# Conv taps copied by transfers into four buffers, one shift sum per slice of the start by moving rows, and four modulation sums side by side, in a two-layer conditioned decoder trunk

## The chip, the cores and the metric

One core of a Trainium2 chip runs the whole program. The metric is device time in microseconds (us) of one execution, the median of three runs; smaller is better. TensorE is called PE (its weight loads PEld), VectorE DVE, ScalarE ACT, GpSimd POOL; SP only issues transfers.

## What is computed

One sequence of 256 tokens (2 tiles of 128), width 1024, two layers. All matrices are float32 and come from HBM once. Every sublayer is modulated: a vector c of 1024 goes through silu and, by `ada_w` (1024 x 9216 for each layer), gives a shift, a scale and a gate for each of the three sublayers.

```python
def swiglu_ffn(h, w_in, w_out):
    u = h @ w_in
    a, b = jnp.split(u, 2, axis=-1)
    return (jax.nn.silu(a) * b) @ w_out

def conformer_conv(h, w_pw1, b_pw1, w_dw, b_dw, ln_g, ln_b, w_pw2, b_pw2):
    u = h @ w_pw1 + b_pw1
    a, g = jnp.split(u, 2, axis=-1)
    u = a * jax.nn.sigmoid(g)
    u = depthwise causal convolution of u over time, 31 taps w_dw, + b_dw
    u = jax.nn.silu(layer_norm(u, ln_g, ln_b))
    return u @ w_pw2 + b_pw2

for i in range(2):
    mod = (silu(c) @ ada_w[i] + ada_b[i]).reshape(B, 3, 3, 1024)
    shift, scl, gate = mod[:, :, 0], mod[:, :, 1], mod[:, :, 2]
    pre = lambda z, j: rms_norm(z, norm_g[i, j]) * (1 + scl[:, j]) + shift[:, j]
    x = x + 0.5 * gate[:, 0] * swiglu_ffn(pre(x, 0), w_in[i, 0], w_out[i, 0])
    x = x + gate[:, 1] * mixer_i(pre(x, 1))        # layer 0: attention, layer 1: conv
    x = x + 0.5 * gate[:, 2] * swiglu_ffn(pre(x, 2), w_in[i, 1], w_out[i, 1])
```

## The kernel before

**Arithmetic.** Every large product is done in three passes of fp32r matmuls: a float32 operand is split into a rounded part (`whi`, `hh`, made by ACT) and a rest (`wlo`, `hl`, made by DVE), and hi*hi, lo*hi and hi*lo are added up in PSUM (`mm3`, L608 to L610).

**The stream.** `plan` writes one list of all weight pieces of 512 KB in the order in which they are used, with pieces of `ada_w` woven in. SP loads them (L203) into a ring of six `raw` buffers. `step` takes one piece: a weight piece is split by ACT (L243) and DVE (L218), a piece of `ada_w` is multiplied by silu(c) on DVE and added up over its rows in an accumulator `acc` of 128 x 512 (L279, L281). Only when a piece has been used is the next load issued. `block` stands before each group of matmuls and runs as many steps as the quota of the stage allows (`PUMP`, in the conv loop `PUMP_LOOP` = 5); `need` runs steps until a certain weight is split. There is no scheduler: each engine runs its instructions in the order in which the code emits them, and waits where an operand isn't there.

**Modulation sums.** A finished `acc` holds half a vector of 1024, still spread over 128 partitions. For a shift or a scale, `column_sum` (L322) sums it with four matmuls whose stationary operand is a 128 x 128 piece of `acc` and whose moving operand is one column of ones; `finish` (L333, L336) adds the bias on DVE. This happens 20 times, for five sublayers, two vectors, two halves. A gate goes through `row_sum` (L312, L313).

**The start.** The shift and scale of the first sublayer are needed at once, in four slices of 256 (`early_fold`, `early_sum`, q = 0 to 3). Of the four pieces of a slice DVE folds three (L477, L479). The fourth, the second half of the shift, goes through PE with the raw weights as the stationary operand (L499, four matmuls of one column for each 128 columns); L500 adds the folded parts.

**The conv.** Eight blocks b of 128 channels. Blocks 0 to 3 are computed with time on the partitions (`UT`, two times each) and turned (`across`), blocks 4 to 7 directly (`U`). `glu(b)` (L1009, L1010) writes 256 time steps of 128 channels into one of three buffers `ub`. `spread(b)` then makes `R[b]`: four groups g of 32 channels, each copied four times, shifted by 0 to 3 steps, onto the four quarters of the partitions; that is 16 copies of 32 x 284 elements, 11 by DVE (L1024) and 5 by ACT (L1022), with two `R` buffers. `wide(b)` (L963, POOL) lays the taps out as 32 x 32 diagonals, with two buffers `wd`. `C(b)` (L1033) is 32 matmuls of 32 output channels each, four groups in four column quarters of the array. `VT` turns the result back, `moments`, `norm` and `swish` do the layer norm and silu, and `O(t, j)` multiplies by `w_pw2`. In the loop over b a turn runs `glu(b+2)`, `C(b)`, `spread(b+2)`, `U(b+4)`, `wide(b+2)`, `VT(b-1)`.

## Time and profile before

| | |
|---|---|
| median of 3 runs | 1071.75 us (1071.41 to 1072.74) |
| the profiled execution's own time | 1072.88 us |
| its span | 1071.0 us |
| PE busy | 1038.3 us (97%) |
| DVE / ACT / POOL busy | 815.1 / 503.8 / 53.2 us |
| read from HBM | 248.24 MB, 233 GB/s over the span |

The span is the time from the first to the last instruction; some 1.9 us lie around it. A busy share is an average over stages: what an instruction is worth is read from its own stage, from what ends the waits there.

### The profile page before, as it was taken

Reading aid. Unit: us, or ns where it says so; the run is one execution under the profiler, and the core shown is the slowest. Engines: PE = TensorE matmul, PEld = TensorE weight load, DVE = VectorE, ACT = ScalarE, POOL = GpSimd, SP = SyncE. Lnnn points to the kernel's source line nnn. Section 1 sums busy time; section 2 is a strip of 40 time slices with the busy share of each in tenths; the row PEclk is TensorE's granted clock in tenths of the full one; section 3 lists DMA queues with packets and bytes.
Section 4 is the critical chain, followed back from the end, with each engine's and each line's share of the span. In section 5 each row is a group of like instructions: output and inputs, shape, how many; then the busy total and the mean of one; then the engine's idle time right before and its main releaser. Section 6 shows DMA issues by size and latency. Waiting matters only on the chain.

```text
span 1071.0 us, 14807 instructions
## 1 busy us (share of the span) xinstructions
PE 1038.3 (97%) x5522; PEld 853.5 (80%) x5522; DVE 815.1 (76%) x1267; ACT 503.8 (47%) x794; POOL 53.2 (5%) x83
## 2 busy tenths in 40 slices
PE   8999999999999999999999999999988799999998
PEld 6888888877777788888878888888867588888886
DVE  5878878878997798778568788776789768665643
ACT  3354444555676544344354444454555446434430
POOL 3000000001210000000020000000211100000000
PEclk8999999999999999999999999999988899999999
DMA  8979998948767399898728889885545227776711
GB/s 297 297 244 340 307 324 296 332 160 260 248 205 221 101 324 313 281 311 293 251 88 311 284 296 317 284 289 159 164 149 195 86 65 238 270 230 199 236 40 39
DMA packets 181692, 250.26 MB, mean 234 GB/s; under 512 B 8389, under 2 KB 132070, under 8 KB 181620
## 3 DMA queue, kind: packets, MB, share of 16 engines
q1 hardware_dynamic: 180784, 248.55, 69.6%
q0 software_dynamic: 688, 0.71, 0.3%
q8 instruction: 43, 0.70, 0.2%
q14 instruction: 29, 0.24, 0.1%
q10 hardware_dynamic: 148, 0.06, 0.0%
HBM read 248.24 MB, written 1.05 MB: 233 GB/s over the span
## 4 chain that ended last, share of the span: by engine, by line
PE 87%; DVE 8%; issue 2%; ACT 1%; DMA 1%; POOL 1%; SPq 0%; DVEq 0%; POOLq 0%; ACTq 0%
PE u L608 15%; PE u L610 15%; PE u L609 14%; PE y L608 11%; PE y L610 11%; PE y L609 11%; DVE R L1024 2%; DVE wlo L218 2%; PE m L686 2%; PE m L322 1%; PE m L1033 1%; DMA raw<-in_ada_w_dram 1%; PE m L499 1%; DVE x L545 1%; PE m L587 1%
## 5 line engine op out<-in xcount | busy, mean ns | idle before, releaser
L218 DVE TENSOR_TENSOR wlo<-raw,whi 128x1024 fp32r<-128x1024 f32 x320 | 382.4, 1224 | 31.2 <-ACT whi L243 31.0
L243 ACT ACTIVATE whi<-raw 128x1024 fp32r<-128x1024 f32 x320 | 328.5, 1054 | 164.2 <-DMA raw<-in_ffn_w_in_dram 97.7
L608 PE MATMUL u<-whi,hh 128*128 128x512 f32 x672 | 266.5, 397 | 0.0
L610 PE MATMUL u<-whi,hl 128*128 128x512 f32 x672 | 262.7, 391 | 0.0
L609 PE MATMUL u<-wlo,hh 128*128 128x512 f32 x672 | 261.8, 390 | 0.0
L281 DVE SCALAR_TENSOR_TENSOR acc<-raw,sc,acc 128x512 f32<-128x512 f32 x224 | 169.5, 757 | 5.6 <-DMA raw<-in_ada_w_dram 0.7
L610 PEld LDWEIGHTS u<-whi,hl 128*128 128x128 f32 x672 | 126.1, 188 | 28.4 <-DVE hl L603 1.2
L608 PEld LDWEIGHTS u<-whi,hh 128*128 128x128 f32 x672 | 126.3, 188 | 25.5 <-ACT hh L602 0.6
L609 PEld LDWEIGHTS u<-wlo,hh 128*128 128x128 f32 x672 | 126.4, 188 | 25.1
L608 PE MATMUL y<-whi,gh 128*128 128x512 f32 x352 | 138.8, 394 | 0.2 <-ACT gh L694 0.2
L610 PE MATMUL y<-whi,gl 128*128 128x512 f32 x352 | 137.3, 390 | 0.0
L609 PE MATMUL y<-wlo,gh 128*128 128x512 f32 x352 | 137.1, 389 | 0.0
L695 DVE TENSOR_TENSOR gl<-m,gh 128x512 fp32r<-128x512 f32 (+1 forms) x48 | 31.1, 647 | 93.0 <-ACT gh L694 92.8
L608 PE MATMUL y<-whi,hh 128*128 128x512 f32 (+1 forms) x256 | 98.2, 384 | 0.0
L609 PE MATMUL y<-wlo,hh 128*128 128x512 f32 (+1 forms) x256 | 94.9, 371 | 0.0
L610 PE MATMUL y<-whi,hl 128*128 128x512 f32 (+1 forms) x256 | 94.7, 370 | 0.0
L694 ACT ACTIVATE gh<-m 128x512 fp32r<-128x512 f32 (+1 forms) x48 | 27.0, 562 | 132.4 <-PE m L686 132.4
L656 ACT ACTIVATE sg<-u 128x256 f32<-128x256 f32 x84 | 32.1, 382 | 113.9 <-PE u L610 113.9
L610 PEld LDWEIGHTS y<-whi,gl 128*128 128x128 f32 x352 | 66.1, 188 | 14.6 <-DVE gl L695 0.4
L608 PEld LDWEIGHTS y<-whi,gh 128*128 128x128 f32 x352 | 66.1, 188 | 13.8 <-ACT gh L694 0.7
L609 PEld LDWEIGHTS y<-wlo,gh 128*128 128x128 f32 x352 | 66.1, 188 | 13.3
L657 DVE TENSOR_TENSOR g<-u,sg 128x256 f32<-128x256 f32 x84 | 35.5, 422 | 35.0 <-ACT sg L656 34.6
(157 smaller groups left out, 984.4 us busy)
## 6 DMA issues: line engine op xcount, KB each, us to landing
raw<-in_ffn_w_in_dram SPq DMA_DIRECT2D x164, 512.0 KB, 5.0
raw<-in_ada_w_dram SPq DMA_DIRECT2D x144, 512.0 KB, 5.0
raw<-in_ffn_w_out_dram SPq DMA_DIRECT2D x88, 512.0 KB, 5.1
raw<-in_attn_w_qkv_dram SPq DMA_DIRECT2D x24, 512.0 KB, 4.8
raw<-in_conv_w_pw_dram SPq DMA_DIRECT2D x24, 512.0 KB, 4.9
raw<-in_ffn_w_in_dram SPq DMA_DIRECT2D x24, 256.0 KB, 5.5
raw<-in_attn_w_o_dram SPq DMA_DIRECT2D x8, 512.0 KB, 4.6
gate<-in_ada_b_dram SPq DMA_DIRECT2D x6, 512.0 KB, 6.7
```

What stands on the lines that cost most here:

```text
L218: (eng or nc.vector).tensor_tensor(lo, raw, hi.bitcast(F32), op=ALU.subtract)
L243: self.nc.scalar.activation(hi, self.like(self.raws[i], hi), AF.Copy)
L281: nc.vector.scalar_tensor_tensor(dst, raw[:, i, :], self.sc[:, k : k + 1], dst, op0=ALU.mult, op1=ALU.add)
L608: nc.tensor.matmul(out, lh, rh, start=start, stop=False)
L609: nc.tensor.matmul(out, lh, rl, start=False, stop=False)
L610: nc.tensor.matmul(out, ll, rh, start=False, stop=stop)
L656: nc.scalar.activation(sg, ps[:, 0:256], AF.Silu)
L657: nc.vector.tensor_tensor(gs[c][:, t, :], ps[:, 256:512], sg, op=ALU.mult)
L686: nc.tensor.transpose(ps[:, o : o + P], g[:, t, k * P : k * P + P], self.ident)
L694: nc.scalar.activation(hi, src, AF.Copy)
L695: nc.vector.tensor_tensor(lo, src, hi.bitcast(F32), op=ALU.subtract)
L1024: nc.vector.tensor_copy(dst, src)
```

## The change

**Conv copies.** `spread` no longer runs on DVE and ACT: the 16 copies of a block become 16 transfers from SBUF to SBUF, eight issued by SP and eight by POOL. `R` and `ub` get four buffers, `wd` three. The order is new: all four of `glu(0..3)`, `spread(0..3)` and `wide(0..2)` stand before the loop, a turn of the loop runs `U(b+4)`, `glu(b+4)`, `C(b)`, `spread(b+4)`, `wide(b+3)`, and the last three blocks are computed for the first 128 time steps before the others. The weights of the conv come first in the stream, the pieces of `ada_w` for (1,2,0) behind them.

**The start.** DVE folds two of the four pieces (the scale). Both pieces of the shift go through PE with silu(c), repeated over 32 columns, as the stationary operand and the raw rows as the moving operand: eight matmuls of 32 x 256 in four column quarters. ACT copies the result (`br`), and two matmuls with the vector `pick` bring it onto the partitions. The two loads of x are issued one piece earlier each.

**Sums.** In the stages up to the third FFN, four finished accumulators are summed together: four matmuls with 32 columns of ones as the stationary operand and `acc` (512 columns) as the moving one, an ACT copy, and two blocks later four transposes (`columns_turn`). There are four such groups of four; the other four sums keep the old form. `acc` has five buffers there. The order of the vectors in the stream changes for this.

```diff
-            vec.acc = self.fp.tile([P, n], F32, name="acc", tag="acc", bufs=2)
+            vec.acc = self.fp.tile([P, n], F32, name="acc", tag="acc", bufs=bufs)
...
-                self.sums.append([3, self.column_sum, vec, dst, c0])
+                self.open.append((vec.number, vec, dst, c0))
+                self.pend.append(self.open[-1])
+                if self.phase > 3 or len(self.pend) == 4:
+                    self.sums.append([3, self.column_sums, self.pend])
+                    self.pend = []
...
+        m = 32 * len(accs)
+        for j, (_, vec, acc, c) in enumerate(accs):
+            nc.tensor.matmul(ps[32 * j : 32 * j + 32, :], self.ones.bitcast(F32)[:, 0:32], acc, start=True, stop=True)
+        rows = self.two.tile([P, 512], F32, name="rows", tag="sq", bufs=1)
+        nc.scalar.activation(rows[0:m, :], ps[0:m, :], AF.Copy)
+        self.sums.append([1, self.columns_turn, accs, rows])
+
+    def columns_turn(self, accs, rows):
...
         for i in range(4):
-            nc.tensor.matmul(ps[:, i : i + 1], acc[:, i * P : i * P + P], self.one, start=True, stop=True)
-        self.finish(vec, ps[:, 0:4], c)
+            nc.tensor.transpose(ps[:, i * P : i * P + m], rows[0:m, i * P : i * P + P], self.ident[0:m, 0:m])
...
+        for e, raw in enumerate(shift):
+            if not q:
                 idle(IDLE_SUMS)
...
+            for k in range(4):
+                nc.tensor.matmul(
+                    rows[32 * k : 32 * k + 32, 0:256], self.sc32[:, 4 * e + k, :], raw[:, k, :],
+                    start=e == 0, stop=e == 1,
+                )
+            self.issue()
+        br = self.two.tile([P, 256], F32, name="br", tag="sq", bufs=1)
+        nc.scalar.activation(br, rows[:, 0:256], AF.Copy)
...
-            R[b] = cp.tile([P, 4, 284], F32, name="R", tag="R", bufs=2)
+            u = ub[b % 4]
+            R[b] = cp.tile([P, 4, 284], F32, name="R", tag="R", bufs=4)
             for g in range(4):
                 for j in range(4):
-                    dst, src = R[b][32 * j : 32 * j + 32, g, :], u[32 * g : 32 * g + 32, j : j + 284]
-                    if 4 * g + j in (1, 4, 7, 10, 13):
-                        nc.scalar.activation(dst, src, AF.Copy)
-                    else:
-                        nc.vector.tensor_copy(dst, src)
+                    eng = nc.sync if (g + j) % 2 else nc.gpsimd
+                    eng.dma_start(R[b][32 * j : 32 * j + 32, g, :], u[32 * g : 32 * g + 32, j : j + 284])
...
-        for b in range(6):
-            if b >= 4:
-                self.block()
-            if b:
-                glu(b + 2)
+        for b in range(4):
+            U(b + 4)
+            glu(b + 4)
             C(b)
...
-            spread(b + 2)
-            if b + 4 < 8:
-                U(b + 4)
-            wide(b + 2)
+            spread(b + 4), wide(b + 3)
...
+        C(4), wide(7), VT(3)
+        self.need(self.pw2[3])
+        take(5)
+        C(5, 0, P), VT(4), self.block(), C(6, 0, P), VT(5, (0,)), C(7, 0, P), VT(6, (0,))
+        C(5, P, P), VT(7, (0,)), moments(0), norm(0, 0), norm(0, 1)
...
-    nc = _bacc.Bacc("TRN2", target_bir_lowering=False, num_devices=1)
+    nc = _bacc.Bacc("TRN2", target_bir_lowering=False, num_devices=1, dynamic_dma_scratch_size=8192)
```

POOL in the conv, from the load of the bias `b` to the powers of the layer norm. Before:

```order
L1100 DMA b_6575<-in_conv_b_pw_dram 128x1024
L963 TENSOR_TENSOR wd<-w_4927,mask 128x1024 x8
L1059 TENSOR_TENSOR lr_7683<-lr_7683,mhalf 128x1
L1059 TENSOR_TENSOR lr_7738<-lr_7738,mhalf 128x1
L564 TENSOR_TENSOR r_7860<-v_7859,mhalf 128x1
```

POOL in the same place, changed:

```order
L1077 DMA R<-ub_6535 32x284 x8
L1077 DMA R<-ub_6532 32x284 x8
L1019 TENSOR_TENSOR wd<-w_4906,mask 128x1024
L1077 DMA R<-ub_6533 32x284 x8
L1019 TENSOR_TENSOR wd<-w_4906,mask 128x1024
L1077 DMA R<-ub_6534 32x284 x8
L1019 TENSOR_TENSOR wd<-w_4906,mask 128x1024
L1077 DMA R<-ub_6535 32x284 x8
L1019 TENSOR_TENSOR wd<-w_4906,mask 128x1024 x2
L1111 TENSOR_TENSOR lr_7646<-lr_7646,mhalf 128x1
```

The eight tap layouts stood alone on POOL; now 64 transfers stand between them, eight ahead of each (the first three blocks, of the same pattern, are left out above), and the layouts of blocks 6 and 7 come last of all.

PE in the second slice of the start (q = 1), between two groups of the FFN's matmuls. Before:

```order
L500 MATMUL m<-one,acc 128x1 x2
L499 MATMUL m<-sc,raw 128x1 x4
L500 MATMUL m<-one,acc 128x1
L499 MATMUL m<-sc,raw 128x1 x4
L500 MATMUL m<-one,acc 128x1
L516 MATMUL m<-ident,z 128x128 x4
L608 MATMUL y<-whi,hh 128x512
```

PE in the same place, changed:

```order
L545 MATMUL m<-raw,sc_158 32x256 x8
L572 MATMUL m<-ident,z 128x128 x4
L535 MATMUL m<-one,acc 128x1 x2
L557 MATMUL m<-pick,br 128x1 x2
L664 MATMUL y<-whi,hh 128x512
```

Twelve matmuls of one column become eight of 256 columns and four of one column; the transposes of z now stand between the row sums and the matmuls that need ACT's copy of them.

## Rows read from the trace of the kernel before

**Rows 1.** The page, part 2: busy tenths of PE in 40 slices

```profile
PE   8999999999999999999999999999988799999998
```

**Rows 2.** Stretches: start:end, length, busy us by engine, PEclk, DMA share, GB/s

```profile
768.00:850.00 82.00, 68.22 (x845) 54.21 (x847) 71.99 (x130) 42.63 (x76) 11.74 (x6) 0.88 0.47 155
850.00:878.90 28.90, 27.37 (x174) 22.57 (x163) 19.25 (x42) 15.00 (x32) 1.66 (x3) 1.00 0.06 19
27.60:40.80 13.20, 13.20 (x69) 11.31 (x68) 11.14 (x22) 4.62 (x6) 0.00 (x0) 0.87 0.96 313
```

**Rows 3.** The chain that ended last, 767 to 856 us: start, us, what

```profile
767.04 0.38 ACT sg L1009
767.44 0.50 DVE ub L1010
...
780.04 0.58 PE u L608
...
852.04 0.64 PE m L1070 x4
...
855.32 0.34 PE y L608
```

**Rows 4.** A group of instructions: line, count | busy, mean ns | idle

```profile
L1024 DVE COPY R<-ub 32x284 f32<-32x284 f32 x88 | 32.6, 370 | 5.4 <-PE m L1033 3.5
```

**Rows 5.** PE in time, 764 to 800 us: start, us, instruction, tile, count

```profile
769.56 0.60 PE L1001 MATMUL u<-ident,z 128*128 128x128 f32 x4
...
788.46 3.66 PE L1033 MATMUL m<-R,wd 128*32 128x256 f32 x64
...
797.91 0.38 PE L1047 MATMUL y<-ident,v 128*128 128x128 f32 x2
```

**Rows 6.** The transfers of the taps, tile tq: ns min/median/max; us to landing

```profile
L931 POOL DMA_DIRECT2D tq<-in_conv_w_dw_dram x8: 551/551/618, 556.9 to 561.3; - x8
...
DMA to landing us min/median/max: 1.9/3.5/4.3
```

**Rows 7.** The stretch of the tap loads, columns as in rows 2

```profile
550.00:560.00 10.00, 10.00 (x50) 8.34 (x49) 8.31 (x14) 5.28 (x11) 3.54 (x8) 1.00 0.21 65
```

**Rows 8.** POOL in time around 830 us: one tap layout

```profile
830.13 1.98 POOL L963 TENSOR_TENSOR wd<-w,mask 128x1024 f32<-128x1024 f32 x1 [8.58 <-PE m L1033]
```

**Rows 9.** DVE in time around 810 and 830 us: two splits each

```profile
810.43 2.36 DVE L218 TENSOR_TENSOR wlo<-raw,whi 128x1024 fp32r<-128x1024 f32 x2
...
830.33 4.00 DVE L218 TENSOR_TENSOR wlo<-raw,whi 128x1024 fp32r<-128x1024 f32 x2
```

**Rows 10.** Transfers by line: issuing queue, KB each, median us to landing

```profile
ab<-in_ada_b_dram POOLq DMA_DIRECT2D x1, 36.0 KB, 5.7
```

**Rows 11.** The output's stores, tile x: ns min/median/max of one issue on SP

```profile
L547 SPq DMA_DIRECT2D out_dram<-x x6: 332/332/344, 1057.9 to 1068.3; - x6
```

**Rows 12.** The chain that ended last, whole span: sums and four transposes

```profile
118.23 0.44 PE m L686 x4
...
144.63 0.79 PE m L322 x8
...
263.68 0.98 PE m L322 x8
```

**Rows 13.** PE and ACT in time in the start, 0 to 56 us

```profile
10.43 1.65 PE L396 MATMUL y<-ones 128*128 128x512 f32 x4
...
16.61 0.56 PE L500 MATMUL m<-one,acc 128*128 128x1 f32 x2
...
27.65 0.50 PE L500 MATMUL m<-one,acc 128*128 128x1 f32 x4
...
28.09 1.06 ACT L243 ACTIVATE whi<-raw 128x1024 fp32r<-128x1024 f32 x1 [1.69 <-DMA raw<-in_ffn_w_in_dram]
...
30.63 0.47 PE L608 MATMUL y<-whi,hh 128*128 128x512 f32 x1
...
31.83 0.63 PE L609 MATMUL y<-wlo,hh 128*128 128x512 f32 x1
```

More of the change, by code (lines that the diff above doesn't have):

```diff
@@ L271, in ada_fold @@
         if k0 == 0:
-            if sum(job[1] == self.column_sum for job in self.sums) > 1:
+            bufs = 2 if self.phase > 3 else 5
+            if any(i <= self.naccs - bufs for i, *_ in self.open):
                 self.run_sums(True)
-            vec.acc = self.fp.tile([P, n], F32, name="acc", tag="acc", bufs=2)
+            vec.acc = self.fp.tile([P, n], F32, name="acc", tag="acc", bufs=bufs)
+            vec.number = self.naccs
+            self.naccs += 1
         dst = vec.acc
@@ L303, in run_sums @@
             job[0] -= 1
+        if force and self.pend:
+            self.sums.append([0, self.column_sums, self.pend])
+            self.pend = []
         while self.sums and (force or self.sums[0][0] < 0):
@@ L467, in early_fold @@
         nc = self.nc
-        accs = []
-        for e in range(3):
+        acc = self.fp.tile([P, 512], F32, name="acc", tag="acc", bufs=5)[:, 0:256]
+        shift = []
+        for e in range(4):
             raw = self.raws[self.taken].rearrange("p (k n) -> p k n", k=4)
-            if e != 1:
-                acc = self.fp.tile([P, 512], F32, name="acc", tag="acc", bufs=2)[:, 0:256]
-                accs.append(acc)
+            self.taken += 1
+            self.high = max(self.high, self.taken)
+            if e >= 2:
+                shift.append(raw)
+                continue
             for i in range(4):
-                k = 4 * (e % 2) + i
+                k = 4 * e + i
                 if k == 0:
@@ L1117, in conv @@
         e = evac(w[1])
-        glu(0), spread(0)
+        glu(0), spread(0), wide(0)
         UT(w[3][:, 256:], 3, 1)
```

124 lines of the change are left out of this document (70 added, 54 removed).

## The prediction

> **What bounds the kernel now.** I read the page's slices first. PE is busy in nine or more tenths of nearly every slice [rows 1]; outside the conv a us that PE doesn't spend is a us of the total, as long as DMA, DVE and ACT keep up. The dip around slice 31 is the conv, and the view by stretch says why: from 768 to 850 us PE works 68.2 of 82.0 us at a mean granted clock of 0.88, while DVE is busy 72.0 [rows 2]. The chain of waits there is a chain of DVE work: `glu` ends at 767.9, and PE's first `U` starts only at 780.04, behind DVE's copies of R, splits and three more `glu` [rows 3]. The copies alone are 32.6 us on DVE [rows 4], and ACT has five a block besides. So in the conv DVE is the bound, and PE pays twice, by waiting and by a lower clock after the waits.
>
> **The conv.** The stretch to compare runs from `glu(0)` (767.44) to the first matmul of O (855.32): 87.9 us [rows 3]. Of the changed order I work out two paths, PE's and POOL's.
>
> PE's path. UT(3,1) ends at 769.56 [rows 5], since nothing ahead of it changes its inputs. Then come ACT's copy of the result, sigmoid (0.38), `glu` (0.50) and the last `across`, which needs the bank that `glu(1)` frees: about 2.3 us, so U(4) starts near 771.9. One U takes 5.79 us (from the end of C at 788.46 + 3.66 to VT at 797.91), one C 3.66, a pair of VT about 0.31 [rows 5]. Four U are 23.2, eight blocks of C 29.3, eight pairs of VT 2.5, at the clock of those rows. The last C would end at 826.9. From the first transposes of `swish` to O it was 3.28 us [rows 3], and this chain stays. O would start at 830.2: a gain of 25.1.
>
> POOL's path. POOL has 64 transfers to issue and eight layouts to write. The nearest row to a transfer from SBUF to SBUF over 32 partitions is the load of the taps, also 32 partitions: 0.551 us of POOL each, landing after 1.9 to 4.3 [rows 6], while DVE was busy 8.3 of 10 us [rows 7]; I take 0.56. A layout is 1.98 [rows 8]. From 767.9 that is 64 x 0.56 + 8 x 1.98 = 51.7: the layout of block 7 is done at 819.6, and only then can C(7) start. Behind its start stand four half blocks (7.3) and VT (0.6): 827.5, so O at 830.8. Both paths end together, so POOL's price decides.
>
> One thing adds to it. With a layout on POOL, a pair of splits on DVE took 4.00 us, without one 2.36 [rows 8, 9]: DVE stood still for most of the layout. The other way round a layout must wait for the split in hand, on average half of 1.2 us; eight times that is 4.9, and O comes at 835.7. By the Trainium skill ("SBUF — State Buffer", SBUF: two separate sides) the engine that starts first holds a port pair shared by DVE and GpSimd for its whole instruction. By that rule the term would be between 0 and 9.8, and the trace agrees with the lock. Between 830.8 and 835.7 I take the middle, 833.2: **a gain of 22 us.**
>
> Bounds. The best is PE's path without any wait, 25. For the worst, POOL's code keeps eight transfers in flight and reuses a slot when the one eight back has landed. A load of 36 KB, the size of one copy (32 x 284 x 4 bytes), landed after 5.7 us on this queue [rows 10]; then a transfer costs 5.7 / 8 = 0.71, 64 x 0.15 = 9.6 more, and the gain is 10 (855.3 - 845.3). 0.56 is nearer, because the tap loads are several in a row over 32 partitions.
>
> What hides the rest. SP issues eight copies a block, about 0.33 us each [rows 11], 2.7 us in a turn of 9.5 (U + C), beside five loads. The first of the eight waits for `glu(b+4)` and for C(b), and all weight loads behind it on SP wait too; the ring of six raw pieces covers that, because the weights of the conv all come ahead of the copies of block 0, and those behind are wanted only at O and in the last FFN. DVE loses 32.6 us of copies in a stage where it was busy 72 of 82, so it is late no more: five splits of 1.2 us and a `glu` are 6.6 in a turn of 9.5. ACT gets five copies a block back. The slower clock goes with the waits it follows: from 850 on, with 1.5 us of idle, it was 1.00 [rows 2].
>
> **The sums.** A sum of one half vector takes PE 0.79 us, in the attention 0.98 [rows 12]. Sixteen sums go, twelve at 0.79 and four at 0.98: 13.4 us. A group of four needs four matmuls of 32 x 512, side by side. C is the same form: 32 matmuls of 256 columns, four abreast, in 3.66, so four of 512 cost 3.66 x 4 / 32 x 2 = 0.91; with four transposes (0.44 [rows 12]) a group is 1.35, four are 5.4. **Gain 8.0.** Were the four not to overlap, a group would be 3.66 + 0.44 = 4.1, a loss of 3; against this stands that C does overlap. ACT's copy of the sums has two blocks of PE work as cover. If that cover went, it would cost ACT's copy, under 1 us for each group. DVE's part is the same as before.
>
> **The start.** In slices 1 to 3 the sums and the transposes of z take PE 2.98 us (27.65 to 30.63 [rows 13]). Now: eight matmuls of 256 columns, 0.91 by the row of C, four transposes 0.44, eight instructions of one column 0.79: 2.14, or 0.8 less each, 2.5 together. Behind the old sums the clock fell: the matmul at 31.83 took 0.63 us [rows 13], and from 27.6 to 40.8 the granted clock is 0.87 [rows 2], 1.7 us lost. The same happens once more, after the last slice. The new sums keep more columns moving, so these 3.4 us may go. But DMA was busy 0.96 of this stretch [rows 2], and ACT's split at 28.09 had waited for its load [rows 13]: loads give a floor that I can't see past. Also PE must wait for ACT's copy `br` behind such a split. In slice 0 the shift saves PE time, but `idle` (1.65 us [rows 13]) now stands twice ahead of the last sums, which ended at 17.2. I take **3 us**, with bounds of -1 (slice 0 later by one idle, nothing else but 0.6) and 7.
>
> **Sum.** 22 + 8 + 3 = 33. The profiled execution took 1072.9 us (span 1071.0 and 1.9 around it); 1072.9 - 33 = 1039.9. The median is 1.1 below the profiled one, so 1038.8, rounded **1039**. The bounds give 1072.9 - 1.1 - (25 + 8 + 7) = 1032 and 1071.8 - (10 + 8 - 1) = 1055.
>
> **The rivals.**
> 1. Loads held back on SP. If the copies' waits for C(b) delay the weights, ACT's splits stand still in front of the sigmoid and of the evacuation of C, which PE needs. Three turns with 5 us each (one landing) take 15 of the conv's 22: 1054. For it: SP works in order. Against it: the ring is six deep and these weights aren't urgent.
> 2. POOL's slots. The change gives the transfers' descriptors an area of 8192 bytes. If it holds only four at a time, a transfer costs 3.5 / 4 = 0.88 [rows 6], 64 x 0.32 = 20.5 on top of 835.7: no gain in the conv is left, and the time is 1061. Against it: the tap loads followed each other at 0.55.
> 3. Slower: POOL's issue waits for DVE. If each issue, like a layout, has to wait for half a split, it costs 0.56 + 0.61 = 1.17; O comes at 835.7 + 39 = 874.7, the conv loses 19, and with 11 gained elsewhere the time is 1080. It decides from 1.04 us a transfer (835.7 + 64 x 0.48 = 866.4, 11 behind the old 855.3). Against it: 0.551 to 0.618 while the tap loads ran beside a busy DVE [rows 6, 7]. The Trainium skill ("SBUF — State Buffer", SBUF: two separate sides) speaks for it: a copy of float32 on DVE keeps GpSimd from writing descriptors, so that a transfer of about 620 ns takes about 3100. The loop of the changed kernel has hardly such copies left; no run here shows how it is with splits.
> 4. The sums don't overlap: 11 us less, 1050.
>
> **How the numbers follow.** Forecast (1030 to 1049) 0.62; rivals 1 and 4 or a slow landing (1049 to 1056) 0.17; rival 2 (1056 to 1069) 0.09; within 0.2%, about what a measurement of this kernel can tell from no change, 0.03; rival 3 0.09. Faster: 0.62 + 0.17 + 0.09 = 0.88. The range leaves out rivals 2 and 3 and the 0.03: 1030 to 1056.
>
> **What would show it.** Right: on POOL, transfers at 0.56 us back to back and the last layout near 820; PE between 772 and 828 nearly without idle at a granted clock near 1.00; O some 22 us earlier relative to the conv's start; four sums in about 0.9 us. Wrong: POOL's issues at 0.7 us or more, C waiting for R or `wd` (rivals 2, 3), ACT waiting for raw loads in the loop (rival 1), PE waiting for `br` or for splits in the first 55 us. A conv that takes as long as before would make the prediction wrong, whatever the sums do.

## The result, and the profile after

The changed kernel takes 1057.4 us in the median of 4 runs (1055.2 to 1060.7), the kernel before 1071.6 beside it: a ratio of 0.987, 95% interval 0.984 to 0.990. That is a gain of 14.2 us where 33 had been forecast, 1.4 us outside the range. Its profiled execution took 1057.27 us, of which 1055.5 is the span.

The slices of the page first (40 equal parts of the span, each digit the busy share in tenths; PEclk is TensorE's granted clock):

```profile
PE   8999999999999999999999999999995899999998
PEclk9999999999999999999999999999998999999999
```

The kernel before has, in the row of the clock:

```profile
PEclk8999999999999999999999999999988899999999
```

The first slice's dip is gone from the clock (9 in place of 8), and PE's hole, 887 in [rows 1], is now 58, in slices 30 and 31. By stretch (busy us of PE, PEld, DVE, ACT, POOL with the number of instructions, then granted clock, DMA share, GB/s):

```profile
0.00:30.00 30.00, 26.69 (x130) 18.58 (x131) 15.69 (x39) 11.73 (x22) 8.70 (x35) 0.94 0.90 302
755.00:800.00 45.00, 43.86 (x511) 35.98 (x513) 27.79 (x24) 14.49 (x22) 34.17 (x53) 1.00 0.67 203
800.00:830.00 30.00, 14.41 (x266) 10.80 (x262) 20.61 (x21) 7.80 (x12) 15.05 (x19) 0.77 0.77 246
```

For 45 us of the convolution PE is nearly never idle at full clock, as forecast. Then, from 800 to 830, it works 14.4 of 30 us, at a clock of 0.77. In that hole lies the gain that didn't come. The waits of the convolution (total us, times, longest) name two late things:

```profile
ACT whi L245 <- DMA raw<-in_ffn_w_in_dram: 24.4, 4, 21.9
ACT whi L245 <- DMA raw<-in_conv_w_pw_dram: 16.6, 3, 14.2
PE y L1099 <- ACT v L1089: 15.0, 2, 11.6
```

ACT's splits wait for raw weights, and PE waits for `v`, the copy of C that stands behind those splits on ACT. From here on three marks tell where the time goes: the first gate (`glu(0)`, written to `ub`), the last gate (block 7), and the first transposes of `swish`, from which the second matrix O follows after some 3 us. The medians are of each kernel's runs, the ratios 95% intervals against the kernel before run beside it. The marks are of one profiled execution each, at most 2.2 us from its kernel's median (hybrid3's is 3.0 above it). In us:

| kernel | median | ratio to before | gate 0 | gate 7 | swish | gate 0 to swish | swish to end of span |
|---|---|---|---|---|---|---|---|
| before | 1071.6 | | 767.4 | 841.0 | 852.0 | 84.6 | 219.0 |
| start_only | 1069.5 | 0.998 to 1.000 | 763.0 | 836.9 | 847.9 | 84.9 | 220.0 |
| conv_old | 1061.6 | 0.990 to 0.993 | 755.4 | 829.5 | 840.5 | 85.1 | 220.0 |
| **changed kernel** | **1057.4** | 0.984 to 0.990 | 755.6 | 813.6 | 836.1 | **80.5** | 219.4 |
| pool_all | 1084.2 | 1.010 to 1.014 | 754.5 | 806.7 | 862.0 | 107.5 | 221.3 |
| pool12 | 1063.2 | 0.991 to 0.994 | 757.0 | 800.4 | 842.5 | 85.5 | 221.0 |
| tiny | 1052.8 | 0.982 to 0.986 | 755.6 | 809.0 | 832.2 | 76.6 | 219.8 |
| half_engines | 1054.1 | 0.983 to 0.986 | 755.2 | 812.1 | 832.1 | 76.9 | 219.3 |
| half_late | 1054.4 | 0.983 to 0.986 | 755.6 | 811.7 | 835.9 | 80.3 | 218.2 |
| pump3 | 1051.9 | 0.981 to 0.984 | 755.5 | 800.0 | 830.9 | 75.5 | 219.4 |
| lean4 | 1059.0 | 0.987 to 0.990 | 755.4 | 806.9 | 831.0 | 75.7 | 226.7 |
| lean2 | 1058.0 | 0.986 to 0.990 | 755.1 | 794.8 | 820.3 | **65.3** | **235.5** |
| half_lean2 | 1060.1 | 0.988 to 0.991 | 755.5 | 803.6 | 822.2 | 66.7 | 235.5 |
| weave_back | 1061.9 | 0.990 to 0.993 | 755.5 | 816.2 | 841.5 | 86.0 | 218.2 |
| act_half | 1060.3 | 0.988 to 0.991 | 755.5 | 816.5 | 838.5 | 83.0 | 219.3 |
| act_half_pump3 | 1050.1 | 0.979 to 0.982 | 755.6 | 807.2 | 828.2 | 72.6 | 221.0 |
| hybrid5 | 1056.9 | 0.985 to 0.988 | 755.8 | 813.9 | 836.0 | 80.2 | 219.7 |
| hybrid3 | 1046.9 | 0.976 to 0.980 | 756.2 | 803.2 | 826.9 | 70.7 | 221.3 |
| **fold_early** | **1044.7** | 0.975 to 0.978 | 754.8 | 794.5 | 825.2 | **70.5** | 217.8 |

steps_late isn't in the table, because its one profiled execution fell into a slow state (1274.5 us at a granted clock of 0.75); its other three have a median of 1058.9, ratio 0.986 to 0.990.

The change brings 11.8 us ahead of gate 0 and only 4.1 between gate 0 and `swish`; behind that nothing changes.

### The profile page after: what moved, and what is told of

It reads as the page before. It is cut to its first block, busy times and chain, and to the rows that moved or that the text cites. A ratio compares the mean times of both kernels' runs of the same rounds, so it can differ in the third digit from the quotient of the medians.

```text
span 1055.5 us, 14925 instructions
## 1 busy us (share of the span) xinstructions
PE 1020.3 (97%) x5510; PEld 826.7 (78%) x5510; DVE 785.3 (74%) x1165; ACT 489.6 (46%) x763; POOL 86.8 (8%) x149
## 4 chain that ended last, share of the span: by engine, by line
PE 79%; DVE 7%; DMA 5%; ACT 3%; issue 3%; POOL 2%; SPq 1%; DVEq 0%; ACTq 0%; POOLq 0%
PE u L666 14%; PE u L664 14%; PE u L665 14%; PE y L664 10%; PE y L666 10%; PE y L665 10%; DMA raw<-in_ffn_w_in_dram 2%; DMA raw<-in_ada_w_dram 2%; DVE wlo L220 2%; PE m L742 2%; ACT whi L245 1%; POOL R L1077 1%; PE m L1085 1%; ACT p L893 1%; DVE x L601 1%
## 5 line engine op out<-in xcount | busy, mean ns | idle before, releaser
L220 DVE TENSOR_TENSOR wlo<-raw,whi 128x1024 fp32r<-128x1024 f32 x320 | 389.2, 1244 | 51.1 <-ACT whi L245 50.8
L666 PEld LDWEIGHTS y<-whi,gl 128*128 128x128 f32 x352 | 66.1, 188 | 14.4 <-DVE gl L751 0.4
L620 POOL TENSOR_TENSOR r<-v,mhalf 128x1 f32<-128x1 f32 x12 | 6.6, 554 | 671.9 <-DVE v L619 671.9
```

The source lines that it names most:

```text
L220: (eng or nc.vector).tensor_tensor(lo, raw, hi.bitcast(F32), op=ALU.subtract)
L666: nc.tensor.matmul(out, ll, rh, start=False, stop=stop)
```

## The experiments

Each is the changed kernel with the edit that is shown, all of them named above. The theories carry the numbers that they have in the expectations: 1, SP's copies make the loads late; 2, the bytes of the copies; 3, the order on ACT alone; 4, POOL; 5, the FFN's splits ahead of C's evacuations; 6, the steps of weights (split or fold) that the stretch is asked for, in front of its gates and evacuations.

### The parts by themselves

conv_old has the function `conv` of the kernel before, with the new order of the stream; start_only takes, on top of that, each sum alone:

```diff
-                if self.phase > 3 or len(self.pend) == 4:
+                if self.phase > 3 or len(self.pend) == 1:
```

> The changed kernel with the convolution of the kernel before put back: what is left is the new start and the sums side by side. My reading of the two traces (theory 1): those two are worth the 11.8 us by which the first gated half is earlier in the changed kernel (767.4 to 755.6), so 1071.6 - 11.8 = 1059.8 us, range 1058 to 1062, and the new convolution is worth only the 2 to 4 us that are left to 1057.4. The sum on record gives -3 for the start and -8 for the sums, 1060.6. Rival: the first 11.8 us come in part from the order of the loads ahead of the convolution, which goes back here with it in nothing but its place; then over 1063. If the new convolution is worth nothing at all, 1057.

> Conv_old with each sum of a half vector taken alone again (four products of one column each, as before), so that of the change only the new start and the five accumulators are left. The sum on record has -3 for the start and -8 for the sums; conv_old is 9.5 us below the kernel before, so by it this is 1067 to 1070. Rival: the start is worth the 6.0 us that the first FFN's end has gained, of which the sums of the first stage can't be much: 1063 to 1066.

Measured: 1061.6 and 1069.5. The start is worth about 2 us (1071.5 to 1069.5; by the ratio 0.2 to 2.6), the sums 7.9 (1069.5 to 1061.6), the new convolution 4.1 (1061.6 to 1057.4). These runs were taken in different sessions; by the ratios, each against the kernel before of its own session, the three are 1.4, 7.7 and 4.9. The rival (1063 to 1066) falls.

### SP's copies moved, or emptied

pool_all starts all sixteen copies of a block on POOL; pool12 twelve; half_engines makes SP's eight on DVE and ACT; tiny leaves them with 4 columns each (pool_all's, half_engines' and tiny's edits):

```diff
-                    eng = nc.sync if (g + j) % 2 else nc.gpsimd
+                    eng = nc.gpsimd
```

```diff
-                    eng = nc.sync if (g + j) % 2 else nc.gpsimd
-                    eng.dma_start(R[b][32 * j : 32 * j + 32, g, :], u[32 * g : 32 * g + 32, j : j + 284])
+                    dst, src = R[b][32 * j : 32 * j + 32, g, :], u[32 * g : 32 * g + 32, j : j + 284]
+                    if (g + j) % 2 == 0:
+                        nc.gpsimd.dma_start(dst, src)
+                    elif 4 * g + j in (1, 6, 11):
+                        nc.scalar.activation(dst, src, AF.Copy)
+                    else:
+                        nc.vector.tensor_copy(dst, src)
```

```diff
-                    eng.dma_start(R[b][32 * j : 32 * j + 32, g, :], u[32 * g : 32 * g + 32, j : j + 284])
+                    n = 4 if (g + j) % 2 else 284
+                    eng.dma_start(R[b][32 * j : 32 * j + 32, g, 0:n], u[32 * g : 32 * g + 32, j : j + n])
```

pool12 has `nc.sync if j == 3 else nc.gpsimd` there. tiny's four buffers `R`, not shown here, are made once and cleared beforehand.

> All sixteen copies of a block are started by POOL and none by SP; bytes, buffers and the order of everything else stay. Theory 1 (SP starts its transfers in order, so its 64 copies hold up the weight loads behind them, and ACT's splits, which stand ahead of the evacuation of C, starve): ACT's waits for raw pieces of weights between 760 and 830 us (41 us in all, longest 21.9 and 14.2) fall under 10 us, and no y of L1099 waits 11 us any more. The time is then POOL's own: 8 blocks of 16 x 0.496 + 1.95 = 9.9 us are 79 us from the first gated half at 755.6, so the last copies land near 836 and the end is 3 to 8 us later than 1057: 1060 to 1065. Theory 2 (it is the bytes of the copies, which take the rings' share from the loads): the waits for raw stay near 40 us. Theory 3 (ACT's order alone): they stay too.

> The eight copies of a block that SP started become copies by engines, five by DVE (0.62 us each) and three by ACT (0.54 each); POOL keeps its eight. Theory 1: no load stands behind a copy any more, ACT's waits for raw pieces from 760 to 830 fall from 41 us to under 10, and the convolution takes about the 66 us of the sum on record plus 2 to 5 for ACT's three copies: 1040 to 1046 us. Theory 2 (bytes): half of the bytes are gone, half of the loss with them: 1048 to 1051. Theory 3 (ACT's splits ahead of the evacuation of C, whatever the loads do): 1054 to 1058. If POOL's transfers bound it (theory 4): no change from 1057 either, with POOL without idle time.

> SP's eight copies of a block carry 4 columns in place of 284, so that the convolution reads zeros where they are left out and the output isn't the reference's; their number, their issue, their queue and their waits stay. Theory 1 (issue and order on SP): within 3 us of the changed kernel, 1054 to 1060, and ACT's waits for raw pieces from 760 to 830 stay over 30 us. Theory 2 (bytes on the wire): the gain that half of the bytes gives, 1040 to 1050, with those waits under 15 us.

> POOL starts twelve of the sixteen copies of a block and SP four. POOL: 8 x (12 x 0.5 + 1.95) = 64 us, as long as its area holds what is under way; with all sixteen it did not, POOL stood 5.7 us at a time for its own transfers to land and the time was 1084. Theory 1: SP has half the copies, so ACT's waits for raw pieces fall from 41 us to 15 to 25. If POOL's area still suffices: 1048 to 1054; if POOL stands for it as before: 1062 to 1075.

Measured. pool_all: 1084.2, far slower than the expected 1060 to 1065. The waits for raw weights are nearly gone (5.1 us), but POOL doesn't start sixteen copies a block without waiting for earlier ones to land. The sum of these waits (us, times, longest), and the chain of waits (start, us, what; a row of DMA is a transfer under way, not a wait of that length):

```profile
POOL R L1077 <- DMA R<-ub: 13.5, 15, 1.7
755.63 1.99 POOL R L1077 x4
757.62 5.73 DMA R<-ub
763.62 1.39 POOL R L1077 x3
```

The start at 763.62 is POOL's thirteenth and follows the landing of the fifth transfer, begun at 757.62: it had waited for the transfer eight back, which is what the prediction's Bounds took for POOL. That the area for descriptors was full, as the expectation of pool12 has it, isn't shown, and its 5.7 us are the time of such a transfer; POOL itself stood at most 1.7 us at a time. The waits move the last copies from the expected 836 to 847; PE waits 16.9 us for layouts, which stand behind the copies on POOL. pool12 still has it, in part (8.8 us in ten waits): 1063.2, inside the second of its two expectations. With eight a block, in the changed kernel, there is none of it.

tiny, nearly without half of the bytes, comes out at 1052.8, between the two expectations: it gains 4.6 us and keeps its waits for raw weights (22.1 and 12.4 us). Those waits don't come from the bytes, so theory 2 falls as their cause; what the bytes cost is 4.6 us at most. Half_engines has nearly none of these waits left (3.3 us in place of 41), as theory 1 wants, and yet gains 3.3 us in place of the expected 11 to 17 (its copies took 0.54 us each on DVE and 0.44 on ACT, less than the 0.62 and 0.54 expected). So late loads were not what kept most of the gain, or something else took their place. At that point I thought that it was DVE, which had been given 40 copies.

### Where the steps stand, and how many

steps_late and half_late write the five steps of a turn behind the turn's gate and evacuation; pump3 asks for three steps a turn in place of five:

```diff
-        take(PUMP_LOOP)
         for b in range(4):
+            take(0)
             U(b + 4)
             glu(b + 4)
             C(b)
             spread(b + 4), wide(b + 3)
+            take(PUMP_LOOP), self.block()
```

```diff
-PUMP_LOOP = 5
+PUMP_LOOP = 3
```

> The changed kernel, transfers and all, with the five steps of a turn (ACT's splits, DVE's remainders and folds, SP's loads behind them) written behind the turn's gate, evacuation of C and spread, in place of in front of them; their number stays. Theory 1, now in two parts: SP's copies make the loads late, and a late load costs PE time only because the split that waits for it stands ahead of the sigmoid and of the evacuation of C on ACT. With the second part gone, PE's waits for v (15 us between 760 and 830) go, ACT's waits for raw pieces stay above 20 us, and the first product of the second matrix comes 12 to 16 us earlier: 1042 to 1047. If the late loads cost the same one stage later (the second matrix's weights, or the first of the last FFN), 1052 to 1058. Theory 2 (the transfers themselves land late): R is waited for by PE, 1055 or more.

> Half_engines (SP's eight copies made by DVE and ACT) with the steps of a turn behind its gate and evacuation, as in steps_late. Half_engines showed DVE busy 97 of 100 from 770 to 820 us, with the gate of block 7 (812.06) behind twelve folds. If that order is what is left: the gates come 8 to 12 us earlier, 1042 to 1047. If DVE's sum of work bounds the stretch, whatever stands first (8 gates, 40 copies, 18 remainders and 16 folds are some 60 us): 1050 to 1054, as half_engines (1054.1).

> Three steps of weights in a turn of the loop in place of five, so eight loads and as many splits or folds move out of the stretch from 760 to 830 into the work behind it. Theory 1: with fewer loads between the copies SP is less late, ACT's waits for raw pieces fall from 41 us under 20 and PE's for v under 6; the convolution ends 6 to 10 us earlier, and the last FFN begins with eight pieces fewer, which costs it 0 to 8: 1047 to 1057. If the folds that move are what the turn behind the convolution waits for, 1058 to 1062.

Measured: 1058.9, 1054.4 and 1051.9. Writing the steps behind the gate gains nothing; by the program's order the steps of turn b then stand in front of the gate of turn b + 1: they are moved by one turn at most. Fewer steps a turn do gain, 5.5 us, though by the program twenty of the changed kernel's twenty-one steps are still asked for before O: with three a turn the gate of block 7 comes at 800.0 in place of 813.6. Theory 3 as I had put it falls. pump3 doesn't decide on theory 1: its time is inside the range that theory 1 gave, but ACT's waits for raw pieces fell only to 26.4 us, not under 20.

### Fewer steps in the stretch

lean4 and lean2 ask for 15 and 9 steps in place of 21 between the entry of the loop and O (two more stand between gate 0 and that entry in all three), the rest behind; weave_back gives the stream back its old order; half_lean2 is lean2 with half_engines' copies. Lean2's edit (lean4 has 4 and 2 in place of 2.25 and 3):

```diff
-PUMP_LOOP = 5
+PUMP_LOOP = 2.25
...
-        self.block()
         C(4), wide(7), VT(3)
...
-        take(5)
-        C(5, 0, P), VT(4), self.block(), C(6, 0, P), VT(5, (0,)), C(7, 0, P), VT(6, (0,))
+        take(0)
+        C(5, 0, P), VT(4), C(6, 0, P), VT(5, (0,)), C(7, 0, P), VT(6, (0,))
...
-        O(0, 0), swish(1, 0), O(0, 1), put(1, 0), swish(1, 1), put(1, 1), take()
+        O(0, 0), swish(1, 0), O(0, 1), put(1, 0), swish(1, 1), put(1, 1), take(3)
...
         O(1, 0), O(1, 1)
+        self.run_sums(True)
         after()
```

> The changed kernel with fewer steps of weights between the first gate and the second matrix: four steps a turn in place of five, none in the tail behind the loop, and two a block (1.6 before) from the third product of the second matrix on. By its program six of the changed kernel's twenty-one steps move behind the convolution, the four of the last FFN's first weights among them; the transfers, SP's eight copies a block among them, stay. Theory 5 (new): what stops PE is that ACT's splits of those FFN weights stand ahead of the evacuations of C, and their loads can't start before the eight pieces of the modulation's weights ahead of them in the ring of six are folded. Then no y waits more than 2 us for v any more, and the second matrix begins 10 to 16 us earlier: 1042 to 1048. Theory 1 (SP's order makes every load late, whichever piece it is): the waits for v stay over 8 us and it gains no more than pump3's 5.5: 1050 to 1057.

> As lean4, but nine steps in the loop (only the second matrix's weights) and three a block from the third product of the second matrix on, so that the eight folds of the modulation's weights (sixteen operations of DVE of 0.77 us and more) move behind the convolution as well. If the folds in front of the gates of blocks 6 and 7 cost what the FFN's splits leave: 2 to 5 us faster than lean4, 1040 to 1045. If they were hidden beside PE's work and are now what the turn behind the convolution waits for: 2 to 8 us slower than lean4.

> The changed kernel with the order of the weight stream as the kernel before had it around the convolution: the eight pieces of the modulation's weights between the convolution's in place of in a row behind them. If it is the row that makes the FFN's first split wait 21.9 us (eight folds in front of its load): that wait falls under 10 us and the time to 1048 to 1053. If it is the number of steps asked of the stretch, not their order: 1055 to 1060.

> Lean2 with SP's eight copies of a block made by DVE (five) and ACT (three), as in half_engines: no load stands behind a copy. If SP's copies still cost time once the steps are out of the way (theory 1 in part): 3 to 8 us faster than lean2. If they don't, DVE's five copies a block (25 us in all) cost and nothing is gained: lean2's time or up to 8 us slower.

Measured: 1059.0, 1058.0, 1061.9, 1060.1. These are misses, and lean2 is the most telling of all. With SP's 64 copies in place, and with nine steps, the convolution takes 65.3 us from gate 0 to `swish`: 19 less than in the kernel before, which is nearly the forecast's 22, and 15.2 less than in the changed kernel. And behind `swish` it takes 235.5 us, 16.1 more than the changed kernel (219.4), so all of that is given back. The stretches of lean2 (columns as above):

```profile
810.00:820.00 10.00, 9.76 (x257) 8.35 (x255) 2.59 (x5) 1.10 (x3) 0.56 (x1) 0.85 0.03 7
820.00:830.00 10.00, 9.01 (x59) 7.23 (x48) 6.39 (x17) 5.56 (x16) 0.55 (x1) 1.00 0.01 2
840.00:850.00 10.00, 2.10 (x15) 2.04 (x14) 8.20 (x14) 5.23 (x8) 0.55 (x1) 0.69 0.58 192
850.00:860.00 10.00, 7.32 (x28) 6.26 (x29) 7.32 (x13) 5.78 (x10) 0.00 (x0) 0.63 0.80 266
```

The DMA share is 0.03 and 0.01 while PE works: the ring of raw pieces is full of modulation weights whose folds stand behind `put` in DVE's order. Then, while DVE makes those folds and the FFN's first weights are loaded, PE is idle 10.6 of 20 us at a clock of 0.63 to 0.69. DVE's timeline of lean2 there (start, us, instruction), and the wait of PE that it ends:

```profile
831.42 0.48 DVE L284 TENSOR_SCALAR acc<-raw,sc 128x512 f32<-128x512 f32 x1
831.93 5.48 DVE L286 SCALAR_TENSOR_TENSOR acc<-raw,sc,acc 128x512 f32<-128x512 f32 x7
837.33 0.48 DVE L284 TENSOR_SCALAR acc<-raw,sc 128x512 f32<-128x512 f32 x1
837.84 2.33 DVE L286 SCALAR_TENSOR_TENSOR acc<-raw,sc,acc 128x512 f32<-128x512 f32 x3
```

```profile
PE m L340 <- DVE acc L286: 7.9, 1, 7.9
```

lean4 is the same in small: 75.7 in the convolution, 226.7 behind. Its y no longer waits for `v`, as theory 5 said, but PE waits 8.5 us for the last layouts (`wd`) and 4.3 for the modulation's sums instead. weave_back is 4.5 us slower than the changed kernel: with the modulation's pieces between the convolution's, ACT waits 35.9 us in ten waits for the convolution's own weights (16.6 in three in the changed kernel). The splits of the FFN's weights wait under 1 us there in place of 24.4, and yet the time is outside both expectations: the new order of the stream is right, and theory 5's "in a row" falls. It also shows that folds aren't the only thing that can lose the stretch: its last turn has none, and its gates 6 and 7 are 9.1 us apart, behind splits that wait for their loads. half_lean2, in which SP starts no copy, is 2 us slower than lean2, with DVE's copies as its price.

The edit of weave_back:

```diff
-        for u in pw1 + pw2:
-            put(u)
-        stream.extend(ada(4, (1, 2, 0)))
+        weave(pw1 + pw2, ada(4, (1, 2, 0)), 3)
```

### Prompt loads without a loaded DVE

act_half makes SP's copies on ACT; hybrid5 does so too, but leaves block 0's with SP and writes the gates of blocks 1 to 3 ahead of their copies; act_half_pump3 and hybrid3 are these with three steps a turn. hybrid5's edit:

```diff
-                    eng = nc.sync if (g + j) % 2 else nc.gpsimd
-                    eng.dma_start(R[b][32 * j : 32 * j + 32, g, :], u[32 * g : 32 * g + 32, j : j + 284])
+                    dst, src = R[b][32 * j : 32 * j + 32, g, :], u[32 * g : 32 * g + 32, j : j + 284]
+                    if (g + j) % 2 == 0:
+                        nc.gpsimd.dma_start(dst, src)
+                    elif b:
+                        nc.scalar.activation(dst, src, AF.Copy)
+                    else:
+                        nc.sync.dma_start(dst, src)
...
-        glu(1), spread(1), wide(1)
+        glu(1)
         across(3, 0, f, 0), across(3, 1, f, 256)
-        glu(2), spread(2), wide(2)
-        glu(3), spread(3)
+        glu(2), glu(3), spread(1), wide(1), spread(2), wide(2), spread(3)
```

> The changed kernel with SP's eight copies of a block made by ACT (0.45 us each in half_engines: 3.6 us a block, 29 us in all, on an engine that is busy 46 of 125 us from 750 to 875 in the changed kernel); POOL keeps its eight, DVE gets none. Theory 1 (SP's copies make the loads late, and that keeps the gain): ACT's waits for raw pieces between 755 and 835 fall from 41 us to under 10, DVE's 13 and 15 us gaps go, and the time is 1042 to 1049, below half_engines (1054). Theory 6 (the amount of steps that the stretch must hold): 1050 to 1056, with PE's waits still there in 800 to 830 or behind it.

> Act_half with three steps a turn in place of five, as pump3 (1051.9 against 1057.4). Theory 1: with the loads prompt the number a turn matters little: within 3 us of act_half. Theory 6: 3 to 6 us faster than act_half, as pump3 was.

> As act_half, but block 0's second half stays with SP, and the gates of blocks 1 to 3 stand ahead of their copies, so that the hole of 7.6 us that act_half has from 760 to 770 us is closed; five steps a turn as in the changed kernel. Theory 1 (late loads): 1042 to 1048. Theory 6 (the five steps a turn, whose folds stand ahead of the gates on DVE and whose splits stand ahead of C's evacuations on ACT, whatever the loads do): act_half's 1060 less the hole, 1052 to 1057, with PE's idle time in 805 to 830.

> Hybrid5 with three steps a turn. Theory 6: 1043 to 1048, that is act_half_pump3's 1050 less most of the hole at the entry, and below hybrid5 by 6 to 10 us. Theory 1: within 3 us of hybrid5.

Measured: 1060.3, 1050.1, 1056.9 and 1046.9. Hybrid5 has no late load left (ACT waits 2.0 us for raw weights) and nothing is gained by it at five steps a turn. Hybrid3 gains 10.0 us over it by the number of steps alone, act_half_pump3 as much over act_half (10.3). Theory 1 says that the number should matter little once loads are prompt; it falls as the main cause. (ACT pays for the copies here: they wait for the gates in its order, and PE waits 15.4 us for `v` behind them in hybrid5.) DVE's timeline of hybrid5 shows what stands in front of the last gate:

```profile
802.54 0.48 DVE L1066 SCALAR_TENSOR_TENSOR ub<-u,cols,sg 128x256 f32<-128x256 f32 x1
...
804.07 1.53 DVE L286 SCALAR_TENSOR_TENSOR acc<-raw,sc,acc 128x512 f32<-128x512 f32 x2
805.51 0.48 DVE L284 TENSOR_SCALAR acc<-raw,sc 128x512 f32<-128x512 f32 x1
806.03 7.96 DVE L286 SCALAR_TENSOR_TENSOR acc<-raw,sc,acc 128x512 f32<-128x512 f32 x7
813.90 0.48 DVE L1066 SCALAR_TENSOR_TENSOR ub<-u,cols,sg 128x256 f32<-128x256 f32 x1
```

Between the gates of blocks 6 and 7 DVE has five folds, ten operations, and works without a gap for 11.4 us, some 2.5 of them beside a layout on POOL (the seven operations took 7.96 us here, 5.48 in the changed kernel). PE needs 9.5 for the U and the C of that turn.

### The folds taken out of the stretch

fold_early leaves transfers, SP's copies and five steps a turn as they are, and reads and folds the last shift's eight pieces in the FFN before:

```diff
-        weave(ffn_order(p2, 0), ada(3, (1, 1, 1), (1, 1, 0), (1, 1, 2), (1, 2, 1)), 4)
+        weave(ffn_order(p2, 0), ada(3, (1, 1, 1), (1, 1, 0), (1, 1, 2), (1, 2, 1), (1, 2, 0)), 4)
...
-        stream.extend(ada(4, (1, 2, 0)))
...
-PUMP = (1.75, 1.8, 1.65, 1.6, 1.6, 1.75)
+PUMP = (1.75, 1.8, 1.65, 1.75, 1.6, 1.75)
```

> The changed kernel with its transfers (SP's eight copies a block among them) and five steps a turn; only the eight pieces of the modulation's last shift, which it folds in the convolution, are read and folded in the FFN before it (1.75 steps a block there in place of 1.6). So 13 steps are left between the first gate and the second matrix in place of 21, and no fold stands ahead of a gate. Theory 6 (steps in front of gates and evacuations): the gate of block 7 comes at about 800 in place of 813.6 relative to a first gate at 755.6, the second matrix begins 70 to 74 us behind the first gate in place of 84, and nothing comes back in the turn to the last FFN; the FFN before pays 0 to 4 us for the folds: 1044 to 1050. Theory 1 (late loads, SP's copies): the waits of ACT's splits for their loads stay and PE still waits 10 us or more for v: 1053 to 1058.

Measured: 1044.7 us, 12.7 below the changed kernel and the fastest of all, ratio 0.976 (0.975 to 0.978). DVE's timeline has the last two gates 5.5 us apart:

```profile
789.01 0.47 DVE L1065 SCALAR_TENSOR_TENSOR ub<-u,cols,sg 128x256 f32<-128x256 f32 x1
789.40 1.21 DVE L1188 TENSOR_TENSOR x<-x,b 128x1024 f32<-128x1024 f32 x1
790.54 4.07 DVE L219 TENSOR_TENSOR wlo<-raw,whi 128x1024 fp32r<-128x1024 f32 x2
794.53 0.47 DVE L1065 SCALAR_TENSOR_TENSOR ub<-u,cols,sg 128x256 f32<-128x256 f32 x1
```

Gate 0 to `swish` is 70.5 us, 10.0 less than in the changed kernel, nothing comes back behind it (217.8), and the FFN that got the folds pays nothing: gate 0 comes 0.8 us earlier. ACT still waits 12.8 us for one of the convolution's weights, as in the changed kernel (14.2), so that wait costs PE little by itself. With the eight folds their eight loads leave the stretch too, and with them the FFN's first weights come in time (ACT waits 2.0 us for them in place of 24.4), so this run alone doesn't part a late gate from a late load. Hybrid5 does, where loads are prompt, the folds stay, and nothing is gained. Together they settle theory 6 for the larger part.

Of the 8.0 us that still lie between 70.5 and the forecast's 62.5 (below), PE's own wait in the same run shows 5.0, and SP's timeline the reason:

```profile
PE m L1084 <- DMA R<-ub: 5.0, 4, 3.5
```

```profile
801.26 6.16 SPq L1076 DMA_DIRECT2D R<-ub  x8
807.52 1.07 SPq L204 DMA_DIRECT2D raw<-in_ffn_w_in_dram  x2
808.96 4.96 SPq L1076 DMA_DIRECT2D R<-ub  x8
```

Block 7's gate is ready at 794.53, and SP starts its eight copies at 808.96, behind those of block 6 and two loads. So theory 1 holds in a smaller size: SP's order costs about 5 us, an estimate from this wait. Two differences agree with it, though both change more than SP's order: lean2, with four loads fewer in the stretch, is 5.2 us shorter there, and hybrid3, which takes most of SP's copies away at three steps a turn, is 5.0 below pump3 in the median. Hybrid3 and fold_early together were not run, so the 5 us are not shown by a run of their own, and the last 3 stay open.

## Why the prediction was wrong

**The sums: right.** 8.0 was forecast, 7.9 measured. A group of four was put at 0.91 for the products and 0.44 for the transposes by the row of C; the changed kernel's chain of waits has

```profile
170.68 1.00 PE m L346 x8
177.35 0.44 PE m L356 x4
```

The four do lie side by side, and rival 4 (if they did not overlap) fell by this row.

**The start: a little too high.** 3 forecast, 0.2 to 2.6 measured, inside the bounds. The clock's dips went as described: 0.94 in the first 30 us, where the kernel before has 0.83, and 1.00 in the next 30 in place of 0.89. The kernel before, then the second stretch of the changed one:

```profile
0.00:30.00 30.00, 25.98 (x112) 21.66 (x113) 18.18 (x41) 11.42 (x19) 8.73 (x35) 0.83 0.89 300
30.00:60.00 30.00, 29.74 (x150) 25.26 (x150) 22.91 (x45) 12.04 (x16) 0.00 (x0) 0.89 0.91 297
30.00:60.00 30.00, 28.77 (x153) 20.75 (x152) 20.31 (x37) 13.96 (x21) 0.00 (x0) 1.00 0.97 316
```

**The convolution: 22 forecast, 4.1 measured.** The two paths that I added up were nearly right. PE's path: gate 0 to `swish` is 65.3 us in lean2, where the sum has 830.2 - 3.3 - 767.4 = 59.5 without any wait and 62.5 at the middle taken. POOL's path, for which the price of a transfer was to decide:

```profile
L1077 POOL DMA_DIRECT2D R<-ub x64: 496/496/532, 756.7 to 818.0; - x64
L1077 SPq DMA_DIRECT2D R<-ub x64: 507/588/1639, 756.2 to 825.3; - x64
```

(least, median and largest ns of the 64 starts on each engine.) POOL's 0.496 is below the 0.56 taken, beside a DVE that was busy 27.8 of 45 us; rivals 2 and 3 fall with it, as long as POOL has eight copies a block. Rival 3 was open for copies on DVE too: in half_engines, with forty of them there, a start took POOL 0.498 us in the median and 0.654 at most.

The step that failed stands under "What hides the rest": "it is late no more: five splits of 1.2 us and a `glu` are 6.6 in a turn of 9.5". Only the first two turns hold nothing but splits, five and two of them, and even the five of the first took 10.6 us, beside two layouts on POOL, where the sum has 6:

```profile
761.08 10.60 DVE L220 TENSOR_TENSOR wlo<-raw,whi 128x1024 fp32r<-128x1024 f32 x5
```

The third turn has three folds of modulation weights among its steps, and in the fourth all five are folds, of two operations of 0.76 to 0.79 us each. With an addition to the residual (1.2) and the gate (0.5) that is 7.8 + 1.2 + 0.5 = 9.5 us, PE's whole turn, before any wait. The changed kernel's DVE in that turn:

```profile
800.11 0.48 DVE L1066 SCALAR_TENSOR_TENSOR ub<-u,cols,sg 128x256 f32<-128x256 f32 x1
800.50 1.22 DVE L1189 TENSOR_TENSOR x<-x,b 128x1024 f32<-128x1024 f32 x1
801.63 1.53 DVE L286 SCALAR_TENSOR_TENSOR acc<-raw,sc,acc 128x512 f32<-128x512 f32 x2
805.80 1.52 DVE L284 TENSOR_SCALAR acc<-raw,sc 128x512 f32<-128x512 f32 x1 [2.64 <-DMA raw<-in_ada_w_dram]
807.36 5.48 DVE L286 SCALAR_TENSOR_TENSOR acc<-raw,sc,acc 128x512 f32<-128x512 f32 x7
813.56 0.48 DVE L1066 SCALAR_TENSOR_TENSOR ub<-u,cols,sg 128x256 f32<-128x256 f32 x1 [0.72 <-ACT sg L1065]
```

The gate of block 7 comes 13.5 us behind that of block 6. I had read DVE's load from the copies that leave it ([rows 4], 32.6 us) and had not written out, turn by turn, what stays. The text on the change said it: it puts the eight pieces, which the kernel before had among the convolution's weights, in a row behind them, and so into the last turns. By the traces both kernels take 23 steps between the first gate and O, but the kernel before has 18 splits and 5 folds there, the changed one 15 and 8.

**The second half of the same step.** "The ring of six raw pieces covers that, because … those behind are wanted only at O and in the last FFN". They are wanted late, but the program asks for them early: ACT's split of the FFN's first piece stands in ACT's order ahead of the evacuation `v` of block 3. ACT's timeline of the changed kernel:

```profile
789.77 0.47 ACT L1089 ACTIVATE v<-m,cols 128x256 f32<-128x256 f32 x1
812.10 1.06 ACT L245 ACTIVATE whi<-raw 128x1024 fp32r<-128x1024 f32 x1 [21.86 <-DMA raw<-in_ffn_w_in_dram]
813.07 0.46 ACT L1065 ACTIVATE sg<-u,cols 128x256 f32<-128x256 f32 x1
813.42 0.47 ACT L1089 ACTIVATE v<-m,cols 128x256 f32<-128x256 f32 x1
```

Its load can be asked for only when the piece six ahead of it, one of the modulation's, is folded, at 800.2; SP starts it at 803.5, behind eight copies and four loads, and the split begins 8.6 us later.

**Rival 1** named this place (ACT's splits in front of the sigmoid and of C's evacuation) and its time, 1054, is near what came. But it gave SP's copies as the reason, and it was held unlikely by the argument about the ring. Of the 18 us between the 62.5 of the sum and the 80.5 measured, fold_early gives the folds and what hangs on them 10.0, and SP's order is put at about 5 by the wait above. Its price for SP was low as well: by the output stores ([rows 11], 0.33 us) I counted 2.7 us for eight copies. They took 0.588 each in the median, and at the entry of the loop the queue reads

```profile
762.46 18.23 SPq L1077 DMA_DIRECT2D R<-ub  x24
780.80 1.51 SPq L205 DMA_DIRECT2D raw<-in_conv_w_pw_dram  x3
```

twenty-four copies in 18.2 us, 0.76 each with SP's waits among them, and three loads of weights behind them. Over the convolution SP also waits 15.6 us, in front of copies, for loads of weights to land (in the kernel before, where it starts no copies, it has no such wait); why a copy waits for a load wasn't followed up. By the Trainium skill ("DMA: Bandwidth & Descriptors", Issuing engines are not separate DMA queues) starting transfers on several engines saves only the time to start them, which is usually small beside the transfer. One start was small here too, 0.588 us on SP beside 3.9 to the landing of such a copy in the median, but 64 of them are 38 us of SP's time in a stretch of 80.5.

**The range.** It ended at 1056, with the bounds of POOL's price and with rivals on single mechanisms. It had no case in which the hidden work, of as many steps as before, fills the shorter turn. lean2 shows that this work can't simply be put off: it leaves eight folds and four splits to the time behind the convolution, and the 15.2 us by which its stretch is shorter are spent there.

## What to carry to other kernels

When a stage is made shorter, list, turn by turn and in program order, the work of each engine that stays in it, and hold its sum against the new turn: work that was hidden in the old one is the next bound, and it comes back wherever it is put next to the end. Of a stage that is shortened by moving work off an engine, first look whether some other stage, with time on that engine, can take what stays; that was worth 12.7 us here, three times the change of the convolution itself. And a queue that loads far ahead is no cover for an engine that is asked, in order, for the farthest of its pieces.

## What the runs showed of the hardware

POOL starts a copy of 32 x 284 within SBUF in 0.496 us (largest 0.532) beside the splits, folds and gates that DVE had in the changed kernel. With eight a block it never waited there for its own copies to land; with twelve it waited 8.8 us in ten waits, with sixteen 13.5 in fifteen. SP took 0.588 us for the same start.

A layout (`wd`) on POOL stops DVE, as in [rows 8, 9], and not splits alone: a fold's first operation, 0.48 us by itself, took 1.52 when it began within a layout, and two splits took 5.51 in place of 2.44, beside two layouts. POOL's timeline of the changed kernel, and under it DVE's:

```profile
805.11 1.92 POOL L1019 TENSOR_TENSOR wd<-w,mask 128x1024 f32<-128x1024 f32 x1
818.56 5.22 POOL L1019 TENSOR_TENSOR wd<-w,mask 128x1024 f32<-128x1024 f32 x2
```

```profile
805.80 1.52 DVE L284 TENSOR_SCALAR acc<-raw,sc 128x512 f32<-128x512 f32 x1 [2.64 <-DMA raw<-in_ada_w_dram]
819.36 5.51 DVE L220 TENSOR_TENSOR wlo<-raw,whi 128x1024 fp32r<-128x1024 f32 x2 [0.19 <-ACT whi L245]
```

POOL's starts of transfers didn't do this to splits: beside five of them, from 788.87, two splits took 2.35 us together.
